# Hybrid decode step: order of the state mixers, their PSUM banks, and a float32 part of the out projection

## The chip, the cores and the metric

The kernel runs on one core of one Trainium2 chip. The metric is the device time of one execution in microseconds (us). The kernel is written with a tile framework: the program text offers instructions with priorities, and a scheduler fixes one static order per engine before the launch. The engines are PE (matrix products), DVE (vector), ACT (scalar functions), POOL (general) and SP (which here issues DMAs).

## The reference

A two-layer hybrid network advances 272 prompt tokens (16 meta tokens and 256) and 8 decode tokens, 280 columns in all. Each layer is a gated feed-forward, then three mixers side by side, then a second feed-forward:

```python
h = x + 0.5 * swiglu(rmsnorm(x, ffn1_norm), ...)
proj = rmsnorm(h, mix_norm) @ w_in
u_s5, p_rwkv, x_lru, g_lru = jnp.split(proj, [...], axis=-1)
o_s5, ...   = s5_group_mixer(u_s5, ...)       # diagonal state space, then a gate z @ glu_w
o_rwkv, ... = rwkv7_group_mixer(p_rwkv, ...)  # S = S*w + sa*(kk*a) + v*k over the tokens, head norm, bonus, gate
o_lru, ...  = rglru_group_mixer(x_lru, g_lru, ...)  # conv of 4, gated linear recurrence, h * gelu(gb)
mix = jnp.concatenate([o_s5, o_rwkv, o_lru], axis=-1) @ w_out
h = h + mix
h = h + 0.5 * swiglu(rmsnorm(h, ffn2_norm), ...)
```

The model width is 1024 (8 row tiles of 128). The mixers' width is 384 for S5 (tiles 0 to 2 of the out projection's rows), 384 for RWKV (tiles 3 to 5) and 256 for RG-LRU (tiles 6 and 7).

## The kernel before

Everything is kept transposed, features on partitions and the 280 tokens on columns. A float32 weight product is made of three faster fp32r matmuls: a weight piece is loaded into a staging buffer (`wpiece`, L180 to L193; five buffers with the tag `stg`), ACT rounds it to `whi` (L191), DVE or POOL takes the remainder `wlo` (L192), and `gemm` (L195 to L203) adds whi·xh, whi·xl and wlo·xh in one PSUM bank, where xh and xl are the same two parts of the activations. PSUM's eight banks are four groups: psa has three, psb two, psc two, psd one. A bank is taken in turn within its group, and the next taker waits until the last has been read.

`mixers` (L1241) runs once per layer. `proj(i)` makes one of 18 tiles of the in projection, 8 x 3 matmuls into a psa bank. In the order of the program text stand:

- RWKV's keys, decay and weighted keys, then `within` for the products EM (i = 0), masked by DVE, one head half in psb and the other in psc;
- `do_i`: the inverses' first stage. `rwkv_inverse` (L902) inverts the triangular 16 x 16 blocks of all chunks on DVE (L922 to L956, between stream transpositions of AD), and yields;
- `do_v`, `do_x`: the values, the bonus and the gate's input;
- `do_o`: `within` again, for the products EO (i = 1);
- `do_s`: three S5 tiles of the in projection and their rearrangement by DMA; `do_l`: four RG-LRU tiles, and the loads of the S5 gate's weights `gw` (tag `stg`);
- `do_C`: `rwkv_chunks` (L1010), a plain function: keys by token, `solve` for the chunks, the inverses' second stage in two groups (L961 to L1008, taken by `next(inv)`), the state over five chunks, the head norms;
- S5's groups and closes (L668, L706) with `do_L` among them: `lru` (L759), conv, two gate products (L777, L780), Tanh, Exp and Sqrt on ACT, the scan (L794), the gelu (L727), the output tile `gb` (L799) and its split in two parts (`split_o`);
- `do_t`: `s5_tail`, three banks of three float32 gate matmuls (L752) on S5's `u`, and their split.

The out projection (L1491 to L1505) then makes eight tiles of rows k = 0, 1, 2, 6, 7 (15 matmuls each, psc) and eight of k = 3, 4, 5 (9 each). DVE adds each into the residual `hres` (L1505), and the second feed-forward begins with its norm.

Of the kernel before, what the change touches and what calls it, by code (L numbers as in the profile page):

```python
# [74 lines left out]
def tile_hybrid_decode(ctx, tc, *args):  # L75
# [683 lines left out]
    def lru(l, mp, cb, gb, s5, pc, hc, out_tile):  # L759
# [28 lines left out]
        for t in range(2):  # L788
# [11 lines left out]
            split_o(6 + t, gb[:, t])  # L800
# [209 lines left out]
    def rwkv_chunks(l, mp, p0, p2, inv, TT, RA, RAw, BK, BK0, EM, EO, vv, vvw, bon, xg, gu, pcl, yd, pc, decode):  # L1010


# [125 lines left out]
        def outputs(c, Tp):  # L1138
# [9 lines left out]
            for hp in range(3):  # L1148
                for h in range(2):
                    yr = slice(64 * h, 64 * h + n)  # L1150
                    PE.matmul(py[yr, hp], EO[:, c, hp, h, 0:n], UV[:, c, hp, h], start=(c == 0), stop=True,
                              skip_group_check=c > 0)
# [3 lines left out]
        st = Tc = out = None  # L1156
        by_token0()
        solve(0)
        next(decode)
        for c, (t0, n) in enumerate(CHUNKS):  # L1160
            if c:

                cs = slice(t0, t0 + n)
                G.tensor_tensor(RA[:, :, :, cs], RA[:, :, :, cs],
                                pcl[:, :, c - 1].unsqueeze(2).unsqueeze(3).to_broadcast([P, 3, 2, n]), op=MUL)
# [3 lines left out]
        keys_by_token(1)  # L1169
# [5 lines left out]
        for c in range(2, 5):  # L1175
            keys_by_token(c)
        for c, (t0, n) in enumerate(CHUNKS):
            bt, uv = bts[c], UV[:, c]
# [57 lines left out]
        return final_state  # L1236
# [4 lines left out]
    def mixers(l, s5, acc, cols, gnext):  # L1241
# [17 lines left out]
        def proj(i):  # L1259
            w = wpiece(w_in[:, :, i * P:i * P + P])  # L1260
            pt = psA()
            gemm(pt[:, :NT], w, ks, xh, xl, ks, True, True)
            return pt
# [27 lines left out]
        def shifted(i, out, ti, act=False):  # L1291

            pt = proj(ti)
# [18 lines left out]
        def decay(hp):  # L1312

            hs = slice(hp * P, hp * P + P)
            pz = psB()
            PE.matmul(pz[:, :NT], lw[0:64, hs], xw[0:64], start=True, stop=True)
            s1 = dk()
            S.activation(s1, pz[:, :NT], AF.Tanh, bias=hc('rwkv_w0', hp), scale=0.5)
            S.activation(s1, s1, AF.Copy, bias=1.0)
            pz = psB()  # L1320
            PE.matmul(pz[:, :NT], lw[64:128, hs], xw[64:128], start=True, stop=True)
            at = dk()
            S.activation(at, pz[:, :NT], AF.Tanh, bias=hc('rwkv_a0', hp), scale=0.5)
# [16 lines left out]
        def keys():  # L1340
# [3 lines left out]
            for hp in range(3):  # L1344
                kt.append(rk())
                shifted(3 + hp, kt[hp], 6 + hp)
                sq.append(rk())
                S.activation(sq[hp], kt[hp], AF.Square, scale=pc('rwkv_k_k', hp))
                for g, m, cs in tok(NT):
                    c = 6 * g + 2 * hp  # L1350
                    PE.matmul(pz[:m, c:c + 2], sq[hp][:, cs], bd1[:, 0:P:64], start=True, stop=True)
# [80 lines left out]
        def do_l():  # L1432
            for t in range(2):
                pt = proj(14 + t)
# [59 lines left out]
        n = cols.stop - cols.start  # L1494
# [100 lines left out]
```

## Time and profile before

| | |
|---|---|
| median of 3 runs | 1278.68 us (1273.01 to 1279.05) |
| profiled execution | 1279.83 us, its span 1278.0 us |
| mean granted PE clock | 0.958 |
| busy, us | PE 1222.5, DVE 999.5, ACT 690.2, POOL 348.9 |
| layer 0, mixers' projections | to 327.9 us |
| layer 0, out projection | 406.5 to 431.3 us |
| layer 1, first S5 gate product of the last five | 1032.1 us |

A row of the timeline gives the start of an instruction in us from the span's start, how long it took, its engine, line and operation with out and in by the program's names, and in brackets the idle time of the engine just before it with the instruction that ended this idle time. Matmuls overlap, so their durations add up to more than the time between their starts. A float32 matmul has two records (x2 is one matmul). The granted clock is a share of PE's full 2.4 GHz; 0.5 is 1.2 GHz.

### The profile page before, as it was taken

The page shows a single profiled execution, that of the slowest core. Times are in us where ns is not written, and L with a number is a line of the kernel's source. Part 1 is how long each engine was busy: PE and PEld are TensorE (multiplying, and loading weights), DVE is VectorE, ACT ScalarE, POOL GpSimd, SP SyncE. Part 2 cuts the span into 40 slices and gives each one's busy share as a digit, 9 for nine tenths or more (in the row PEclk, how much of TensorE's full clock was granted, in tenths as well). Part 3 has the DMA queues.
Part 4 walks back from the last instruction along what each step waited for, and adds up shares of the span by engine and source line. Part 5 has one row for each costly group of instructions (what it writes and reads, how often), then busy time and mean ns, then how long its engine had stood idle before and what let it go on. Part 6 is the DMA issues. An engine that isn't in the chain of part 4 may idle for free.

```text
span 1278.0 us, 29512 instructions
## 1 busy us (share of the span) xinstructions
PE 1222.5 (96%) x10744; PEld 1161.3 (91%) x10744; DVE 999.5 (78%) x2395; ACT 690.2 (54%) x1489; POOL 348.9 (27%) x619
## 2 busy tenths in 40 slices
PE   7999899999898999989999999999999989999997
PEld 6999899988776999989998999998888779999996
DVE  7999976679687799998667878756876778987854
ACT  4556565564355555656544555556633656555552
POOL 2104852033443210385207000001615332500000
PEclk9999999989897999989999999999995989999998
DMA  7665455524311756535578665654333028866662
GB/s 187 168 182 156 132 148 154 164 83 117 92 33 50 187 160 190 156 104 169 161 185 225 194 171 167 178 168 142 105 86 93 3 83 223 237 193 177 179 187 79
DMA packets 376911, 187.49 MB, mean 147 GB/s; under 512 B 45532, under 2 KB 375352, under 8 KB 376766
## 3 DMA queue, kind: packets, MB, share of 16 engines
q1 hardware_dynamic: 376430, 184.47, 52.0%
q8 instruction: 84, 1.38, 0.4%
q10 hardware_dynamic: 336, 1.15, 0.3%
q14 instruction: 61, 0.50, 0.1%
HBM read 181.31 MB, written 3.37 MB: 145 GB/s over the span
## 4 chain that ended last, share of the span: by engine, by line
PE 79%; DVE 11%; DMA 4%; issue 2%; ACT 2%; POOL 1%; SPq 0%; DVEq 0%; ACTq 0%; POOLq 0%
PE psa L202 11%; PE psa L201 11%; PE psa L200 10%; PE psc L201 6%; PE psc L202 6%; PE psc L200 6%; PE psb L202 6%; PE psb L200 6%; PE psb L201 6%; DVE wlo L192 3%; DMA stg<-in_ffn_w_gate_dram 2%; DMA stg<-in_ffn_w_up_dram 1%; PE psc L752 1%; PE psc L677 1%; PE psc L715 1%
## 5 line engine op out<-in xcount | busy, mean ns | idle before, releaser
L191 ACT ACTIVATE whi<-stg 128x512 fp32r<-128x512 f32 (+2 forms) x664 | 399.3, 608 | 354.4 <-PE psa L201 116.1
L192 DVE TENSOR_TENSOR wlo<-stg,whi 128x512 fp32r<-128x512 f32 (+2 forms) x640 | 445.8, 700 | 129.0 <-PE psa L202 35.3
L202 PE MATMUL psa<-xh,wlo 128*128 128x280 f32 (+1 forms) x930 | 275.7, 298 | 5.0 <-DVE wlo L192 4.5
L200 PE MATMUL psa<-xh,whi 128*128 128x280 f32 (+1 forms) x930 | 273.7, 295 | 2.8 <-DVE ts L1296 2.1
L201 PE MATMUL psa<-xl,whi 128*128 128x280 f32 (+1 forms) x930 | 272.9, 294 | 0.0
L202 PEld LDWEIGHTS psa<-xh,wlo 128*128 128x128 f32 x930 | 176.4, 190 | 10.4 <-DVE wlo L192 7.9
L200 PEld LDWEIGHTS psa<-xh,whi 128*128 128x128 f32 x930 | 177.5, 191 | 5.4 <-DVE ts L1296 2.3
L201 PEld LDWEIGHTS psa<-xl,whi 128*128 128x128 f32 x930 | 177.0, 190 | 1.8 <-issue 1.0
L202 PE MATMUL psc<-xh,wlo 128*128 128x280 f32 (+1 forms) x498 | 145.1, 292 | 1.8 <-DVE wlo L192 1.8
L200 PE MATMUL psc<-xh,whi 128*128 128x280 f32 (+1 forms) x498 | 145.2, 292 | 1.0 <-ACT xh L264 0.5
L201 PE MATMUL psc<-xl,whi 128*128 128x280 f32 (+1 forms) x498 | 144.8, 291 | 1.1 <-DVE xl L265 0.7
L202 PE MATMUL psb<-xh,wlo 128*128 128x280 f32 (+1 forms) x396 | 115.6, 292 | 1.3 <-DVE wlo L192 1.3
L200 PE MATMUL psb<-xh,whi 128*128 128x280 f32 (+1 forms) x396 | 115.8, 292 | 0.2 <-ACT whi L191 0.2
L201 PE MATMUL psb<-xl,whi 128*128 128x280 f32 (+1 forms) x396 | 115.3, 291 | 0.0
L202 PEld LDWEIGHTS psc<-xh,wlo 128*128 128x128 f32 x498 | 94.0, 189 | 2.8 <-DVE wlo L192 2.7
L200 PEld LDWEIGHTS psc<-xh,whi 128*128 128x128 f32 x498 | 94.0, 189 | 2.3 <-ACT xh L738 0.8
L201 PEld LDWEIGHTS psc<-xl,whi 128*128 128x128 f32 x498 | 94.0, 189 | 1.9 <-DVE xl L265 1.0
L202 PEld LDWEIGHTS psb<-xh,wlo 128*128 128x128 f32 x396 | 74.9, 189 | 2.2 <-DVE wlo L192 2.2
L200 PE MATMUL psb<-hh,whi 128*128 128x280 f32 (+1 forms) x264 | 76.7, 291 | 0.0
L200 PE MATMUL psa<-hh,whi 128*128 128x280 f32 (+1 forms) x264 | 76.6, 290 | 0.0
L202 PE MATMUL psb<-hh,wlo 128*128 128x280 f32 (+1 forms) x264 | 76.5, 290 | 0.0
L202 PE MATMUL psa<-hh,wlo 128*128 128x280 f32 (+1 forms) x264 | 76.5, 290 | 0.0
(618 smaller groups left out, 2743.3 us busy)
## 6 DMA issues: line engine op xcount, KB each, us to landing
stg<-in_ffn_w_gate_dram SPq DMA_DIRECT2D x176, 256.0 KB
stg<-in_ffn_w_up_dram SPq DMA_DIRECT2D x176, 256.0 KB
stg<-in_ffn_w_down_dram SPq DMA_DIRECT2D x160, 256.0 KB
stg<-in_w_in_dram SPq DMA_DIRECT2D x72, 256.0 KB
stg<-in_w_out_dram SPq DMA_DIRECT2D x32, 192.0 KB
bc<-ds SPq DMA_DIRECT2D x24, 192.0 KB
stg<-in_ffn_w_down_dram SPq DMA_DIRECT2D x32, 128.0 KB
bc<-ds SPq DMA_DIRECT2D x12, 256.0 KB
```

What stands on the lines that cost most here:

```text
L191: S.activation(hi[:, :kc], st[:, :kc], AF.Copy)
L192: (eng or V).tensor_tensor(lo[:, :kc], st[:, :kc], hi[:, :kc].bitcast(F32), op=SUB)
L200: PE.matmul(out, w[wk[i]][0], ah[:, k], start=(first and i == 0), stop=False)
L201: PE.matmul(out, w[wk[i]][0], al[:, k], start=False, stop=False)
L202: im = PE.matmul(out, w[wk[i]][1], ah[:, k], start=False, stop=(last and i == n - 1))
L677: PE.matmul(px[r][:, a], s5['xbt'][:, 4 * T + a, r], u4[:, 4 * T + a, 8:16 + NQ], start=True, stop=True)
L715: PE.matmul(py[32 * i:32 * i + 32, c0:c0 + n], w, x[:, o:NQ + ND], start=(m == 0), stop=(m == 2), skip_group_check=True, tile_position=(0, ...
L752: PE.matmul(pz[:, :NT], gw[k][:, j], z5[:, k, 0:NT], start=(k == 0), stop=(k == 2))
```

## The change

It has three parts.

First, `rwkv_chunks` becomes a generator in three pieces. Its first piece (chunk 0's keys and solution, the inverses' second stage, chunk 1's solution, the values by token) is offered right behind `do_x`, ahead of `do_o`, `do_s` and `do_l`. Its second piece (decode, the other keys, chunks 0 to 2) is offered behind `do_o`. Its last piece (chunks 3 and 4, the head norms) is offered behind `do_t`, in a block of high priority. The scaling of RA by pcl is split in the two kinds of rows, so that each stands where its kind is needed.

Second, the S5 and RG-LRU projections and the third key tile take psc banks instead of psa banks, and the decay takes both its psb banks before it reads the first.

Third, RG-LRU's rows of the out projection (k = 6, 7) are made by plain float32 matmuls from `gb` and unsplit weights: four tiles `ow` with the tag `stg` are loaded in `do_l` by eight DMAs of 128 KB, and ahead of `do_t` sixteen matmuls (L1510) and eight adds into `hres` (L1511) take the place of 48 fp32r matmuls. The loop of the out projection then has k = 0, 1, 2 and k = 3, 4, 5, each tile with one weight piece, and DVE takes every remainder. `gb` is not split any more.

```diff
@@ lru
             V.scalar_tensor_tensor(gb[:, t], gb[:, t], 0.5, h, op0=MUL, op1=MUL)
-            split_o(6 + t, gb[:, t])
@@ rwkv_chunks
         by_token0()
         solve(0)
-        next(decode)
-        for c, (t0, n) in enumerate(CHUNKS):
-            if c:
-
-                cs = slice(t0, t0 + n)
-                G.tensor_tensor(RA[:, :, :, cs], RA[:, :, :, cs],
-                                pcl[:, :, c - 1].unsqueeze(2).unsqueeze(3).to_broadcast([P, 3, 2, n]), op=MUL)
+        enter(0)
         for w in range(2):
             values_by_token(w)
             first_by_token(w)
-        keys_by_token(1)
         next(inv)
         solve(1)
         next(inv)
         for w in range(2, 5):
             values_by_token(w)
-        for c in range(2, 5):
+        yield
+        next(decode)
+        enter(1)
+        for c in range(1, 5):
             keys_by_token(c)
         for c, (t0, n) in enumerate(CHUNKS):
+            if c == 3:
+                yield
...
@@ mixers
-        def proj(i):
+        def proj(i, bank=psA):
             w = wpiece(w_in[:, :, i * P:i * P + P])
-            pt = psA()
+            pt = bank()
...
-            pz = psB()
+
+            pz, pa = psB(), psB()
             PE.matmul(pz[:, :NT], lw[0:64, hs], xw[0:64], start=True, stop=True)
+            PE.matmul(pa[:, :NT], lw[64:128, hs], xw[64:128], start=True, stop=True)
...
-                shifted(3 + hp, kt[hp], 6 + hp)
+                shifted(3 + hp, kt[hp], 6 + hp, bank=psC if hp == 2 else psA)
...
-                pt = proj(14 + t)
+                pt = proj(14 + t, psC)
...
-                pt = proj(16 + t)
+                pt = proj(16 + t, psC)
                 V.scalar_tensor_tensor(gb[:, t], pt[:, :NT], KR, rs, op0=MUL, op1=MUL)
+
+            R['lw'] = [wp.tile([P, 4, P], F32, name="ow", tag="stg", bufs=NBW[0]) for _ in range(KD // 2)]
+            for i, w in enumerate(R['lw']):
+                for q in range(2):
+                    nc.sync.dma_start(w[:, 2 * q:2 * q + 2], w_out[:, 6:8, (2 * i + q) * P:(2 * i + q) * P + P])
             R['gw'] = glu_weights(l)
...
-                pt = proj(T)
+                pt = proj(T, psC)
...
         do_x()
+        chain = do_C()
+        next(chain)
         do_o()
+        next(chain)
         do_s()
         do_l()
-        do_C()
...
         s5_close(s5, u5, R['u4'], 2, R['2'])
+
+        n = cols.stop - cols.start
+        for j in range(KD):
+            pt = psC()
+            for k in range(2):
+                PE.matmul(pt[:, :n], R['lw'][j // 2][:, 2 * (j % 2) + k], gb[:, k, cols], start=(k == 0), stop=(k == 1))
+            V.tensor_tensor(hres[:, j, cols], pt[:, :n], hres[:, j, cols], op=ADD)
         do_t()
+        with tc.high_priority():
+            next(chain)
...
-        OPE = [G, G, V]
-        for kk in ([0, 1, 2, 6, 7], [3, 4, 5]):
-            rw = len(kk) == 3
+        for kk in ([0, 1, 2], [3, 4, 5]):
+            rw = kk[0] == 3
...
-                w = wpiece([w_out[:, 3:6, js]] if rw else [w_out[:, 0:3, js], w_out[:, 6:8, js]], V if rw else OPE[j % len(OPE)])
+                w = wpiece(w_out[:, kk[0]:kk[0] + 3, js])
```

PE around the start of the inverses' second stage (the first L970), layer 0. In the kernel before all projections stand ahead of these rows; psa, psb, psc and psd are the bank groups, L1046 brings values and keys to token rows, L677 are S5's groups, L1087 is chunk 0's solution:

```order
L177 MATMUL psa<-ident,BK_3697 16x64
L177 MATMUL psa<-ident,vv 16x64
L970 MATMUL psb<-AD,EM 32x16 x12
L677 MATMUL psc<-u_4597,xbt 128x76 [waits DMAHW4_49,DMAHW3_49,DMAHW5_49,DMAHW2_49,Pool_49]
L677 MATMUL psc<-u_4597,xbt 128x76 [waits DMAHW6_49,DMAHW7_49,DMAHW1_49,DMAHW0_49]
L1046 MATMUL psa<-ident,vv 128x128 [waits DVE_49]
L1046 MATMUL psa<-ident,vv 128x128 x2
L677 MATMUL psc<-u_4597,xbt 128x76 [waits DMAHW4_49,DMAHW5_49,DMAHW3_49,DMAHW2_49]
L677 MATMUL psc<-u_4597,xbt 128x76 [waits DMAHW6_49,DMAHW7_49,DMAHW1_49,DMAHW0_49]
L677 MATMUL psc<-u_4597,xbt 128x76 x4
L1087 MATMUL psd<-UV,EM 16x64 [waits Activation_49]
```

And in the changed kernel, where the second stage is at L969, the transpositions at L1047 and chunk 0's solution at L1088:

```order
L202 MATMUL psc<-xh,wlo 128x280
L969 MATMUL psb<-AD,EM 32x16 [waits DVE_49,Activation_49]
L969 MATMUL psb<-AD,EM 32x16 [waits Activation_49]
L969 MATMUL psb<-AD,EM 32x16 x3
L1047 MATMUL psa<-ident,RA 128x128 [waits Activation_49]
L1088 MATMUL psd<-UV,EM 16x64 [waits Activation_49]
L1047 MATMUL psa<-ident,RA 128x128
L1088 MATMUL psd<-UV,EM 16x64 [waits Activation_49]
L1088 MATMUL psd<-UV,EM 16x64 x4
L1047 MATMUL psa<-ident,RA 128x128
L1047 MATMUL psa<-ident,vv 128x128 x3
L1047 MATMUL psa<-ident,RA 128x128 x3
```

The second stage now stands behind two S5 tiles (48 matmuls in psc, the last of them in the first row) and ahead of the other five (120 matmuls, the first of which follows two rows further down), and S5's groups come behind all of these.

DVE at the end of RG-LRU's chain, layer 0, before. L727 is the gelu, L799 writes `gb`, L739 splits it, and L1127 to L1133 and the lines with smy and smd are head norms:

```order
L1127 SCALAR_TENSOR_TENSOR bon<-psa,pv,bon 128x64 [waits PE_49]
L1127 SCALAR_TENSOR_TENSOR bon<-psa,pv,bon 128x64 x2
L163 TENSOR_TENSOR smyrt<-smyry 128x3 [waits DVE_49]
L165 SCALAR_TENSOR_TENSOR smdrt<-smdrt 128x24 [waits DVE_49]
L799 SCALAR_TENSOR_TENSOR gb<-gb,tf 128x280
L727 SCALAR_TENSOR_TENSOR gb<-tf,gb 128x280 [waits Activation_49]
L1131 TENSOR_TENSOR bon<-bon,vv 128x3x64 [waits DVE_49]
L164 TENSOR_TENSOR smyrt<-smyrt,smyv 128x3 [waits DVE_49]
L166 SCALAR_TENSOR_TENSOR smdry<-smdrt,smdry 128x24 [waits DVE_49]
L727 SCALAR_TENSOR_TENSOR u_4121<-tf 128x280 [waits Activation_49]
L799 SCALAR_TENSOR_TENSOR gb<-gb,tf 128x280 [waits DVE_49]
L739 SCALAR_TENSOR_TENSOR xl<-gb,xh 128x280 [waits Activation_49]
```

And in the changed kernel, where L1132 and L1134 are the last rows of the head norms and L1511 the new adds:

```order
L1134 TENSOR_TENSOR xl<-bon,xh 128x3x72 [waits Activation_49]
L790 SCALAR_TENSOR_TENSOR ta<-tf,ta 128x280 [waits Activation_49] x2
L792 SCALAR_TENSOR_TENSOR tf<-tf 128x280 [waits Pool_49]
L794 SCALAR_TENSOR_TENSOR tf<-tf 128x272 [waits DVE_49]
L792 SCALAR_TENSOR_TENSOR tf<-tf 128x280 [waits Pool_49]
L794 SCALAR_TENSOR_TENSOR tf<-tf 128x272 [waits DVE_49]
L727 SCALAR_TENSOR_TENSOR gb<-tf,gb 128x280 [waits Activation_49]
L799 SCALAR_TENSOR_TENSOR gb<-gb,tf 128x280 [waits DVE_49]
L727 SCALAR_TENSOR_TENSOR gb<-tf,gb 128x280 [waits Activation_49]
L799 SCALAR_TENSOR_TENSOR gb<-gb,tf 128x280 [waits DVE_49]
L727 SCALAR_TENSOR_TENSOR u_4121<-tf 128x280 [waits Activation_49]
L1511 TENSOR_TENSOR hres<-psc,hres 128x280 [waits PE_49] x8
```

The steps of RG-LRU's chain from L790 on stand alone, behind all head norms, where they were mixed with them before.

PE from RG-LRU's output to the out projection, layer 0, before. L752 are the S5 gate's products, L175 and L177 transpose outputs of the head norms, L200 is the first matmul of the out projection:

```order
L752 MATMUL psc<-u_4121,gw 128x280 [waits DMAHW4_49,DVE_49]
L752 MATMUL psc<-u_4121,gw 128x280
L752 MATMUL psc<-u_4121,gw 128x280 [waits Activation_49]
L752 MATMUL psc<-u_4121,gw 128x280 x2
L175 MATMUL psa<-ident,EM 64x64 [waits DVE_49]
L177 MATMUL psa<-ident,EM 64x64
L175 MATMUL psa<-ident,EM 64x64
L177 MATMUL psa<-ident,EM 64x64
L175 MATMUL psa<-ident,EM 64x64
L177 MATMUL psa<-ident,EM 64x64
L200 MATMUL psc<-xh,whi 128x280 [waits Activation_49]
L201 MATMUL psc<-xl,whi 128x280 [waits DVE_49]
```

And in the changed kernel, where the first row is the last pair's first of the sixteen L1510:

```order
L1510 MATMUL psc<-gb,ow 128x280 [waits DMAHW5_49,DVE_49]
L1510 MATMUL psc<-gb,ow 128x280
L752 MATMUL psc<-u_4121,gw 128x280 [waits DMAHW6_49,DVE_49]
L752 MATMUL psc<-u_4121,gw 128x280 [waits DMAHW7_49]
L752 MATMUL psc<-u_4121,gw 128x280 [waits DMAHW0_49]
L752 MATMUL psc<-u_4121,gw 128x280 [waits DVE_49]
L752 MATMUL psc<-u_4121,gw 128x280 x2
L752 MATMUL psc<-u_4121,gw 128x280 [waits Activation_49]
L752 MATMUL psc<-u_4121,gw 128x280 x2
L200 MATMUL psc<-xh,whi 128x280 [waits Activation_49]
L201 MATMUL psc<-xl,whi 128x280 [waits DVE_49]
```

All sixteen float32 matmuls stand ahead of all nine of L752 (four of which stood further up before), and no transposition is left among them. On SP, the eight loads of `ow` stand where the first pieces of the out projection's weights were: the loads of the second and third `gw` and of all those pieces now stand behind a wait for PE, which is done with `ow` at L1510.

## Rows read from the trace of the kernel before

**Rows 1.** The page, part 1: busy us, share of the span, instructions.

```profile
PE 1222.5 (96%) x10744; PEld 1161.3 (91%) x10744; DVE 999.5 (78%) x2395; ACT 690.2 (54%) x1489; POOL 348.9 (27%) x619
```

**Rows 2.** The page, part 4: the chain that ended last, by engine.

```profile
PE 79%; DVE 11%; DMA 4%; issue 2%; ACT 2%; POOL 1%; SPq 0%; DVEq 0%; ACTq 0%; POOLq 0%
```

**Rows 3.** Busy time by stretch; columns stand in the first line, stretches in us.

```profile
core 0: us, PE busy (x) PEld busy (x) DVE busy (x) ACT busy (x) POOL busy (x), PEclk, DMA share, GB/s
303.00:327.90 24.90, 24.90 (x199) 23.17 (x197) 21.91 (x58) 7.12 (x12) 5.98 (x9) 1.00 0.25 64
327.90:361.50 33.60, 28.90 (x658) 24.41 (x657) 23.48 (x55) 13.45 (x41) 16.92 (x30) 0.80 0.39 106
361.50:406.50 45.00, 39.27 (x555) 28.17 (x553) 35.98 (x116) 28.59 (x72) 17.35 (x27) 0.81 0.06 17
406.50:431.30 24.80, 24.46 (x187) 24.01 (x187) 16.31 (x40) 14.82 (x33) 6.96 (x8) 1.00 0.58 166
957.00:1005.00 48.00, 46.83 (x876) 39.92 (x876) 29.43 (x68) 20.58 (x62) 22.86 (x41) 0.61 0.26 72
```

**Rows 4.** PE timeline: start, duration, line, operation, count, idle before it and its releaser.

```profile
249.66 0.93 PE L285 MATMUL psd<-ident,nrm 128*128 128x128 f32 x6
...
251.64 0.40 PE L200 MATMUL psa<-xh,whi 128*128 128x280 f32 x1 [1.05 <-DVE ts L1296]
...
330.45 0.38 PE L970 MATMUL psb<-AD,EM 16*32 16x16 f32 x24
...
361.04 0.52 PE L1046 MATMUL psa<-ident,vv 128*64 128x128 f32 x3
...
381.68 0.74 PE L777 MATMUL psc<-tf,lg 128*128 128x280 f32 x2
...
382.26 0.64 PE L780 MATMUL psc<-tf,lg 128*128 128x280 f32 x2
...
400.41 4.85 PE L752 MATMUL psc<-u,gw 128*128 128x280 f32 x10 [2.44 <-DVE u L727]
...
406.48 0.40 PE L200 MATMUL psc<-xh,whi 128*128 128x280 f32 x1
...
880.85 0.40 PE L200 MATMUL psa<-xh,whi 128*128 128x280 f32 x1 [1.05 <-DVE ts L1296]
...
1032.11 4.74 PE L752 MATMUL psc<-u,gw 128*128 128x280 f32 x10 [2.76 <-DVE u L727]
```

**Rows 5.** DVE timeline, same columns.

```profile
302.40 0.67 DVE L192 TENSOR_TENSOR wlo<-stg,whi 128x512 fp32r<-128x512 f32 x1
...
303.00 1.08 DVE L922 STREAM_TRANSPOSE wk<-AD 128x512 f32<-128x512 f32 x1
...
312.42 1.71 DVE L943 TENSOR_TENSOR wk<-DD,XI 128x512 f32<-128x512 f32 x1
...
322.74 1.10 DVE L955 STREAM_TRANSPOSE AD<-wk 128x512 f32<-128x512 f32 x1
...
400.27 0.44 DVE L799 SCALAR_TENSOR_TENSOR gb<-gb,tf 128x280 f32<-128x280 f32 x1
...
433.78 0.44 DVE L1505 TENSOR_TENSOR hres<-psc,hres 128x280 f32<-128x280 f32 x1
...
1031.98 0.43 DVE L799 SCALAR_TENSOR_TENSOR gb<-gb,tf 128x280 f32<-128x280 f32 x1
...
1064.64 0.43 DVE L1505 TENSOR_TENSOR hres<-psc,hres 128x264 f32<-128x264 f32 x1
```

**Rows 6.** DVE alone by stretch: busy time, clock, DMA share, GB/s.

```profile
303.00:400.35 97.35, 76.52 (x207) 0.87 0.22 57
361.50:400.35 38.85, 31.13 (x95) 0.84 0.04 11
```

**Rows 7.** ACT timeline, RG-LRU gates of layer 0.

```profile
382.93 0.49 ACT L781 ACTIVATE tf<-psc,h 128x280 f32<-128x280 f32 x1
...
385.00 1.28 ACT L787 ACT_TABLE_LOAD   x1
...
386.30 0.76 ACT L787 ACTIVATE ta<-ta 128x280 f32<-128x280 f32 x2
```

**Rows 8.** DVE groups by line and form, layer 0 mixers: busy, mean ns, idle before.

```profile
L1127 DVE SCALAR_TENSOR_TENSOR bon<-psa,pv,bon 128x64 f32<-128x64 f32 x6 | 1.3, 278 | 1.7 <-PE psa L177 1.7
```

More of the change, by code (lines that the diff above doesn't have):

```diff
@@ L1008, in rwkv_inverse, with rwkv_chunks @@
             yield
-    def rwkv_chunks(l, mp, p0, p2, inv, TT, RA, RAw, BK, BK0, EM, EO, vv, vvw, bon, xg, gu, pcl, yd, pc, decode):
+    def rwkv_chunks(l, mp, p0, R, inv, TT, RA, RAw, BK, BK0, EM, vv, vvw, bon, xg, gu, pcl, yd, pc, decode):
+        p2 = R['p2']
         UV = p0.tile([P, 5, 3, 2, 64], F32, name="UV", tag="uv")
@@ L1150, in outputs @@
                     yr = slice(64 * h, 64 * h + n)
-                    PE.matmul(py[yr, hp], EO[:, c, hp, h, 0:n], UV[:, c, hp, h], start=(c == 0), stop=True,
+                    PE.matmul(py[yr, hp], R['EO'][:, c, hp, h, 0:n], UV[:, c, hp, h], start=(c == 0), stop=True,
                               skip_group_check=c > 0)
@@ L1156, in rwkv_chunks, with enter @@
         st = Tc = out = None
+        def enter(i):
+            for c, (t0, n) in enumerate(CHUNKS):
+                if c:
+                    cs = slice(t0, t0 + n)
+                    G.tensor_tensor(RA[:, :, i, cs], RA[:, :, i, cs],
+                                    pcl[:, :, c - 1].unsqueeze(2).to_broadcast([P, 3, n]), op=MUL)
         by_token0()
         solve(0)
-        next(decode)
-        for c, (t0, n) in enumerate(CHUNKS):
-            if c:
-                cs = slice(t0, t0 + n)
-                G.tensor_tensor(RA[:, :, :, cs], RA[:, :, :, cs],
-                                pcl[:, :, c - 1].unsqueeze(2).unsqueeze(3).to_broadcast([P, 3, 2, n]), op=MUL)
+        enter(0)
         for w in range(2):
@@ L1234, in final_state @@
             nc.sync.dma_start(D['p_rwkv'][l][0].rearrange("(a h) v k -> (h v) a k", h=2), sf)
-        return final_state
+        R['fs'] = final_state
+        yield
     NU = 12
@@ L1289, in mixers, with shifted @@
         dst_ = mp.tile([P, 15, ND], F32, name="dst", tag="sd")
-        def shifted(i, out, ti, act=False):
-            pt = proj(ti)
+        def shifted(i, out, ti, act=False, bank=psA):
+            pt = proj(ti, bank)
             pb = tmp("s", 4, p1)
@@ L1319, in decay @@
             S.activation(s1, s1, AF.Copy, bias=1.0)
-            pz = psB()
-            PE.matmul(pz[:, :NT], lw[64:128, hs], xw[64:128], start=True, stop=True)
             at = dk()
-            S.activation(at, pz[:, :NT], AF.Tanh, bias=hc('rwkv_a0', hp), scale=0.5)
+            S.activation(at, pa[:, :NT], AF.Tanh, bias=hc('rwkv_a0', hp), scale=0.5)
             af = dk()
@@ L1465, in do_C @@
             G.tensor_copy(vd, vv[:, :, NPR:NT])
-            R['fs'] = rwkv_chunks(l, mp, p0, R['p2'], R['inv'], R['TT'], RA, RAw, BK, BK0, EM, R['EO'], vv, vvw, bon, xg, gu, pcl, yd, pc,
-                        rwkv_decode(l, mp, ds, vv, dots, ys, yd))
+            return rwkv_chunks(l, mp, p0, R, R['inv'], R['TT'], RA, RAw, BK, BK0, EM, vv, vvw, bon, xg, gu, pcl, yd, pc,
+                               rwkv_decode(l, mp, ds, vv, dots, ys, yd))
         def do_L():
@@ L1488, in mixers @@
         s5_close(s5, u5, R['u4'], 2, R['2'])
+        n = cols.stop - cols.start
[4 more added lines that the diff above has]
+            V.tensor_tensor(hres[:, j, cols], pt[:, :n], hres[:, j, cols], op=ADD)
         do_t()
+        with tc.high_priority():
+            next(chain)
         ro, rc = R['ro'], R['rc']
         acc2 = new_acc()
-        n = cols.stop - cols.start
-        OPE = [G, G, V]
-        for kk in ([0, 1, 2, 6, 7], [3, 4, 5]):
-            rw = len(kk) == 3
+        for kk in ([0, 1, 2], [3, 4, 5]):
+            rw = kk[0] == 3
             if rw:
```

## Prediction

> **What bounds the kernel now.** I read the page's first part and the chain before anything else: PE is busy 96% of the span [rows 1] and the chain that ended last lies on it for 79% [rows 2]. That average hides the only stretch that the change touches, so the next view is the table by stretches [rows 3]. In layer 0's mixers, from 327.9 to 406.5 us, PE still counts as busy, but with small products, and at a granted clock of 0.80 and 0.81: the projections have ended and nothing large is left to fill it. DVE there is busy 23.48 of 33.60 and 35.98 of 45.00 us. From 406.5 the out projection runs dense at clock 1.00: 192 matmuls of 280 columns in 24.80 us, 0.129 each. Layer 1 is colder: 0.61 from 957 to 1005.
>
> The single instructions show what that stretch waits for. PE's order has the last projection at 327.9, the inverses' second stage from 330.45, the last of its values at about 361.5, then five gate matmuls (L752) from 400.41, released by DVE's `u`, and the out projection at 406.48 [rows 4]. On DVE, the inverses' first stage lasts from 303.00 to about 323.8, and RG-LRU's second output tile `gb` is written by 400.71 [rows 5]. Between 303.00 and 400.35 DVE is busy 76.52 of 97.35 us, in the last part 31.13 of 38.85 [rows 6]. So this stretch is a chain DVE, PE, ACT, DVE in which DVE has most of the work, and its end, `gb` and `u`, opens the out projection. A gain needs that end earlier by more than the tail behind it gets longer.
>
> **Third key tile in an own bank.** PE waits 1.05 us at 251.64 for a bank, behind the norm's transposes at 249.66 [rows 4]; another bank lets these 24 matmuls run there. -1.0 us per layer (0 to -1.05). The decay's two banks cost nothing on the path: the rows show no PE wait there, and the cover is the projections beside it.
>
> **Earlier first stage.** In the new order two splits (0.6 apart) and one S5 evacuation (0.65) no longer stand ahead of the first transposition: it starts at 303.00 - 1.85, about 301.2 [rows 5]. Six splits (3.6), three evacuations (1.8) and 0.4 of idle leave its 20.8 us: AD is ready at about 301.2 + 14.9 = 316.1, where before PE reached it at 330.45.
>
> **PE behind it.** The S5 tiles now use the two psc banks that hold the EO products. DVE frees these in its own order, behind 1.71 us multiplies such as that at 312.42 [rows 5]. So PE stands from about 302 to 308.5, runs 48 matmuls (6.2) to 314.7 and waits 1.4 more for AD. Since AD comes last, I count the wait for the banks as nothing; were AD early or the masks later, it would cost up to its 6.5 us per layer, which is a rival below. The Trainium skill (Perfetto Trace Analysis, Matmuls) says that independent matmul groups should rotate through different PSUM banks so that the evacuation of one overlaps the next group's matmuls; here seven tiles lose three banks for two shared ones, so it speaks against this part, and by it alone the sum would be 1303.5 instead of 1290.5. Behind AD 120 matmuls follow (15.5 us at 0.129), with some 14.5 us of second stage, solves and transposes, about half of the 28.90 that PE spends between 327.9 and 361.5 [rows 3]; S5's groups are the other half. The last projection and the inverses end at 316.1 + 30.0, about 346.2: 15 us before the 361.5 of now.
>
> **What DVE still owes.** The order has 23 more instructions between the first transposition and the last `u` than before: two splits, one S5 evacuation, the last chunk's bonus products and small norm steps, which stood ahead or behind. At 1.4 for the splits and about 0.18 for each of the others that is 5.2 us, so 76.5 + 5.2 = 81.7. What stands ahead of the last projection's evacuation is 33.5 of it. S5's groups, the chunks, the head norms and RG-LRU, 48.2 us, now all come behind 346.2. Idle comes on top. RG-LRU's gates for the second tile stand behind all head norms on PE, ACT and DVE, so nothing covers their latency any more: 1.2 on PE (381.68 to 382.9 [rows 4]), 4.1 on ACT from 382.93 to 387.06, a table load of 1.28 among it [rows 7], and some 1.2 of POOL: 6.5 us. For the chunks and norms I keep 4.1, about half of the 7.7 that DVE idles from 361.50 to 400.35 [rows 6]; the waits for the bonus transposes, 1.7 in one group alone [rows 8], are of this kind. `gb` is ready at 346.2 + 48.2 + 10.6, about 405.0 to 405.2, against 400.71: **+4.5 us**. Layer 1 lies 629.2 later by its key tile (880.85 against 251.64 [rows 4]): 1034.4, where its cold stretch now gives 1032.41 [rows 5]: **+2.0**. The bounds: no idle but RG-LRU's 6.5, filled from the start, gives 301.2 + 81.7 + 6.5 = 389.4; twice the chunks' idle gives 409.3.
>
> **The tail behind `gb`.** Before, it takes from 400.71 to the last add into `hres`, which ends at 434.22: 33.5 us in layer 0; in layer 1 from 1032.41 to 1065.07, 32.7 [rows 5]. Now the sixteen float32 matmuls stand ahead of all gate matmuls and can't start before `gb`. One takes 0.97 at the low clock (five in 4.85 at 400.41) and half, 0.49, at the high one; a pair at 381.68 shows 0.58 [rows 4]. PE has waited long before them, so I take four at 0.97 and twelve at 0.49: 9.8. Bounds: 7.8 (all at the high clock) and 15.5 (none). Nine gate matmuls follow, 4.5; the wait for the first split of their output, 1.4 (1.2 lie between 405.26 and 406.48 now [rows 4], with transpositions in them); 144 matmuls, 18.6; to the end of the last add 2.9, as from 431.3 to 434.22 now. Sum 37.2: +3.7 in layer 0. In layer 1, with 264 columns, the sixteen, the 144 and the rest come to about 36.4, again **+3.7**. The 48 matmuls removed (6.2 us) are worth less than the sixteen cost, and of the nine gate matmuls, four of which had run before 400.41, all stand behind `gb` now.
>
> **Off the path.** ACT loses eight weight splits and the two of `gb`; DVE gets eight adds and all lo-parts, and loses those two tiles' lo-parts; POOL loses six splits. DVE is busy 16.31 of 24.80 us in the out projection [rows 3], which covers them. On SP eight 128 KB loads go into four of the five staging buffers, and two gate tiles and the out projection's first weights wait until the sixteen matmuls free them. The first weights then have 10 us until the out projection; I cost that at 0, and up to 2 us per layer if landing, split and remainder take longer.
>
> **Sum.** Layer 0: -1.0 + 4.5 + 3.7 = 7.2. Layer 1: -1.0 + 2.0 + 3.7 = 4.7. Together 11.9 on the profiled execution's 1279.83: 1291.7. That execution stands 1.15 above the median of the runs, so 1290.5 us.
>
> **Rivals.** *DVE's holes fill: faster.* S5 and RG-LRU work beside the chunks, with no idle but RG-LRU's latency. That puts `gb` 15.8 earlier than forecast: -8.6 in layer 0, -11.1 in layer 1, 1260 profiled. It decides at 7.2 of the 15.8 in layer 0; at three quarters (11.9 each) the time is 1267.9, or 1266.7 against the median. For it: 20.8 us of idle are there [rows 6], and PE is free. Against: S5's first group is offered only behind the last projection, and the RG-LRU tail is alone. The Trainium skill (Perfetto Trace Analysis, Optimization Strategy) says that where the most-contended engine changes over time, interleaving these regimes may improve the time. Here the projections (PE) and the inverses (DVE) are such regimes; no row of the kernel before shows them interleaved.
>
> *It cancels.* Half of the 15.8 is saved, 7.9 per layer: 1279.83 + 11.9 - 15.8 = 1275.9, 1274.8 against the median; between a third and a half it is within the noise, so I put this case at 1278.
>
> *The wait for the banks counts.* The EO masks come behind AD's transposition or the first stage ends sooner, and PE's 6.5 us move everything behind: 1291.7 + 13.0 = 1304.7, 1303.5 against the median. For it: the 1.71 us multiplies [rows 5]; against: the masks stand ahead of AD's transposition in DVE's order.
>
> *A cold, starved tail: slower still.* All sixteen at the low clock (+5.7 per layer) and weights 1.5 late: 11.9 + 14.4, 1306 profiled, 1305. For it: 0.61 in layer 1's stretch [rows 3] and five cold gate matmuls in both layers (1032.11 too [rows 4]). That the change does not do what it says is excluded by the order of its instructions.
>
> **How the numbers follow.** The forecast has 0.42, with its own range from 1285 to 1300. The holes filling has 0.22 (1258 to 1272), the cancelling case 0.22 (1272.3 to 1285), the wait for the banks 0.04, the cold tail 0.10. About 0.5% (6.4 us) is what a measurement of this kernel tells from no change; so faster 0.22, same 0.22, slower 0.56. The range reaches from 1264 to 1305: it leaves out some 0.08 below and 0.06 above.
>
> **What would show it.** Right: PE idle near 302 to 308 behind the EO products; the second stage starting at about 316; the last projection at about 346; `gb` at 404 to 406 less the shift of the key tile; DVE waits in the last 10 us before it; sixteen matmuls in 9 to 11 us, and 37 us from `gb` to the last add. Wrong: `gb` before 396, or a tail under 34 us.

## The result and the profile after

The changed kernel takes 1318.28 us (median of 4 runs, 1317.47 to 1320.09) against 1277.43 for the kernel before in 4 runs: a ratio of 1.033 by the record (95% interval 1.0304 to 1.0356; the two medians alone give 1.032). The profiled executions differ by 1317.99 - 1279.83 = 38.2 us. The forecast was slower by 11.9, 1290.5 us, and 1318 lies above its range of 1264 to 1305: the direction held, the size did not.

From the page's first two parts: the first row is the changed kernel's and answers to [rows 1]. The clock rows, 40 slices of the span, are the changed kernel's and then that of before. They show where the clock falls: slices 9 to 13 and 29 to 33, the mixers of the two layers, in most of them lower than before.

```profile
PE 1231.5 (94%) x10712; PEld 1165.6 (89%) x10712; DVE 1009.1 (77%) x2415; ACT 684.2 (52%) x1469; POOL 325.5 (25%) x603
...
PEclk9999999987875999999999999999888779999998
...
PEclk9999999989897999989999999999995989999998
```

The table by stretches of the changed kernel, layer 0, with the columns of [rows 3]:

```profile
303.00:318.00 15.00, 15.00 (x85) 13.44 (x84) 14.52 (x38) 4.88 (x10) 0.42 (x1) 0.66 0.07 19
318.00:331.00 13.00, 13.00 (x199) 11.38 (x200) 7.65 (x23) 6.75 (x18) 1.65 (x5) 1.00 0.42 111
331.00:353.80 22.80, 22.80 (x408) 21.34 (x408) 10.56 (x26) 3.60 (x11) 3.50 (x8) 0.78 0.40 106
353.80:394.20 40.40, 34.49 (x591) 28.05 (x590) 30.76 (x82) 16.21 (x45) 18.86 (x34) 0.84 0.10 27
394.20:421.20 27.00, 12.09 (x124) 8.25 (x125) 15.84 (x64) 13.44 (x27) 7.02 (x13) 0.56 0.03 6
421.20:459.10 37.90, 35.83 (x206) 30.54 (x205) 25.65 (x60) 18.75 (x43) 0.00 (x0) 0.94 0.47 137
```

Two stretches stand out. From 303 to 318 PE gets through 85 records only, at clock 0.66, and few weights arrive (19 GB/s). The same stretch before:

```profile
303.00:318.00 15.00, 15.00 (x123) 13.41 (x122) 14.18 (x41) 4.59 (x8) 3.96 (x4) 1.00 0.28 77
```

From 394 to 421 DVE is busy 15.84 of 27.00 us and PE 12.09, at clock 0.56: up to 407 the last head norms with RG-LRU's conv, then the rest of RG-LRU's chain alone. The end of the mixers was cold before too (0.55 from 390 to 406.5), but there DVE was busy 13.99 of 16.50 us. The first stretch is also in SP's waits of the changed kernel, 300 to 330 us (total, times, longest). Weight loads stand 19.3 us behind one split, so the weight buffers were full and nothing drained them; before, the longest such wait is 7.1 us and all of them 14.0.

```profile
SPq L188 <- DVE wlo L192: 25.0, 4, 19.3
```

PE and DVE of the changed kernel, layer 0, columns of [rows 4]:

```profile
251.65 0.93 PE L285 MATMUL psd<-ident,nrm 128*128 128x128 f32 x6
...
310.17 0.60 PE L200 MATMUL psc<-xh,whi 128*128 128x280 f32 x1
...
317.90 0.29 PE L969 MATMUL psb<-AD,EM 16*32 16x16 f32 x10
...
351.72 0.76 PE L1003 MATMUL psa<-TT,Z 32*32 32x32 f32 x36
...
407.12 1.27 PE L777 MATMUL psc<-tf,lg 128*128 128x280 f32 x2 [2.10 <-DVE tf L773]
...
420.43 10.48 PE L1510 MATMUL psc<-gb,ow 128*128 128x280 f32 x32 [8.14 <-ACT tf L726]
...
430.74 4.41 PE L752 MATMUL psc<-u,gw 128*128 128x280 f32 x18
...
436.02 0.40 PE L200 MATMUL psc<-xh,whi 128*128 128x280 f32 x1 [0.87 <-ACT ta L754]
```

```profile
302.89 1.06 DVE L921 STREAM_TRANSPOSE wk<-AD 128x512 f32<-128x512 f32 x1
...
315.49 1.14 DVE L954 STREAM_TRANSPOSE AD<-wk 128x512 f32<-128x512 f32 x1
...
354.09 0.45 DVE L1451 SCALAR_TENSOR_TENSOR gb<-psc,nry 128x280 f32<-128x280 f32 x1 [0.65 <-PE psc L202]
...
393.19 0.92 DVE L1128 SCALAR_TENSOR_TENSOR bon<-psa,pv,bon 128x144 f32<-128x144 f32 x3 [3.80 <-PE psa L177]
...
412.25 0.81 DVE L790 SCALAR_TENSOR_TENSOR ta<-tf,ta 128x280 f32<-128x280 f32 x2 [4.58 <-ACT ta L787]
...
419.39 0.45 DVE L727 SCALAR_TENSOR_TENSOR gb<-tf,gb 128x280 f32<-128x280 f32 x1 [2.75 <-ACT tf L726]
...
420.72 0.45 DVE L799 SCALAR_TENSOR_TENSOR gb<-gb,tf 128x280 f32<-128x280 f32 x1
...
458.69 0.44 DVE L1528 TENSOR_TENSOR hres<-psc,hres 128x280 f32<-128x280 f32 x1
```

In what follows times are counted from the mixers' norm (the transpositions at 249.66 before [rows 4], 251.65 now), since its place varies between runs, 247.5 to 253.5 us over all kernels here, with the same program ahead of it. From the norm to the last add into the residual, layer 0 now takes 207.5 instead of 184.6 us and layer 1 201.1 instead of 186.2: 22.9 + 14.9 = 37.8, the whole loss.

| us behind the norm, layer 0 (layer 1) | before | after |
|---|---|---|
| first transposition of AD starts | 53.3 (50.9) | 51.2 (51.5) |
| inverses' second stage starts | 80.8 (78.4) | 66.2 (66.8) |
| inverses end | 109.4 (111.1) | 100.8 (100.0) |
| last projection evacuated | 78.8 (76.4) | 102.9 (102.1) |
| RG-LRU's second output tile written | 151.0 (153.6) | 169.5 (165.5) |
| last add into the residual | 184.6 (186.2) | 207.5 (201.1) |

The inverses do come 9 to 11 us earlier. The projections of S5 and RG-LRU come 24 to 26 later, and RG-LRU's output and the last add are late with them.

One count will be needed below: how many matmuls L201 (one of the three fp32r products; a tile has eight) run between the first transposition of AD and the last evacuation of a projection. It is a row of the view by stretches for that line alone (length, busy, count, clock, DMA share, GB/s). Before:

```profile
303.00:328.47 25.47, 13.30 (x45) 1.00 0.25 63
```

After, where 56 is all seven S5 and RG-LRU tiles (in the kernel before, 11 of the 56 had run ahead of the first transposition):

```profile
302.89:354.54 51.65, 18.14 (x56) 0.80 0.30 80
```

### The profile page after: what moved, and what is told of

It is laid out like the page before. It is cut to its first block, busy times and chain, and to the rows that moved or that the text cites. A ratio compares the mean times of both kernels' runs of the same rounds, so it can differ in the third digit from the quotient of the medians.

```text
span 1316.3 us, 29422 instructions
## 1 busy us (share of the span) xinstructions
PE 1231.5 (94%) x10712; PEld 1165.6 (89%) x10712; DVE 1009.1 (77%) x2415; ACT 684.2 (52%) x1469; POOL 325.5 (25%) x603
## 5 line engine op out<-in xcount | busy, mean ns | idle before, releaser
L202 PE MATMUL psa<-xh,wlo 128*128 128x280 f32 (+1 forms) x802 | 234.2, 293 | 2.2 <-DVE wlo L192 2.0
L200 PE MATMUL psa<-xh,whi 128*128 128x280 f32 (+1 forms) x802 | 234.6, 293 | 0.7 <-ACT whi L191 0.7
L201 PE MATMUL psa<-xl,whi 128*128 128x280 f32 (+1 forms) x802 | 232.5, 291 | 0.0
L200 PE MATMUL psc<-xh,whi 128*128 128x280 f32 (+1 forms) x594 | 177.5, 300 | 3.9 <-ACT ta L754 1.8
L201 PE MATMUL psc<-xl,whi 128*128 128x280 f32 (+1 forms) x594 | 176.3, 297 | 1.9 <-DVE xl L265 1.0
L202 PE MATMUL psc<-xh,wlo 128*128 128x280 f32 (+1 forms) x594 | 176.0, 297 | 1.8 <-DVE wlo L192 1.8
L202 PEld LDWEIGHTS psa<-xh,wlo 128*128 128x128 f32 x802 | 150.7, 188 | 5.6 <-DVE wlo L192 4.6
L200 PEld LDWEIGHTS psa<-xh,whi 128*128 128x128 f32 x802 | 151.4, 189 | 3.5 <-issue 2.2
L201 PEld LDWEIGHTS psa<-xl,whi 128*128 128x128 f32 x802 | 151.1, 189 | 0.8 <-issue 0.7
L200 PEld LDWEIGHTS psc<-xh,whi 128*128 128x128 f32 x594 | 114.5, 193 | 7.1 <-ACT ta L754 2.7
L201 PEld LDWEIGHTS psc<-xl,whi 128*128 128x128 f32 x594 | 115.0, 194 | 3.2 <-DVE xl L739 1.8
L200 PE MATMUL psb<-xh,whi 128*128 128x280 f32 (+1 forms) x396 | 115.0, 291 | 0.0
L201 PE MATMUL psb<-xl,whi 128*128 128x280 f32 (+1 forms) x396 | 114.8, 290 | 0.0
L200 PE MATMUL psb<-hh,whi 128*128 128x280 f32 (+1 forms) x264 | 76.8, 291 | 0.0
L200 PE MATMUL psa<-hh,whi 128*128 128x280 f32 (+1 forms) x264 | 76.6, 290 | 0.0
L201 PE MATMUL psb<-hl,whi 128*128 128x280 f32 (+1 forms) x264 | 76.6, 290 | 0.0
```

Source lines behind the costliest of these rows:

```text
L200: PE.matmul(out, w[wk[i]][0], ah[:, k], start=(first and i == 0), stop=False)
L201: PE.matmul(out, w[wk[i]][0], al[:, k], start=False, stop=False)
L202: im = PE.matmul(out, w[wk[i]][1], ah[:, k], start=False, stop=(last and i == n - 1))
```

## The experiments

Each run gives its median time, its ratio to the kernel before as run beside it, and in brackets the 95% interval of that ratio. Times "behind the norm" are of layer 0 unless both layers are given.

Theory A: the last chunk piece's priority pushes RG-LRU's chain behind the head norms. Theory B: projections among the inverses' second stage are what costs, by way of the banks. Theory C: the float32 products. Later ones are D (late projections, whatever made them late), F (psc shared with EO) against G (the chunks in pieces), and H (the turn of the banks keeps the tiles from filling PE's holes) against I (two banks are too few).

### Four parts taken out or alone

**e1**, the changed kernel:

```diff
-        with tc.high_priority():
-            next(chain)
+        next(chain)
```

> The changed kernel with the last piece of the RWKV chunks (chunks 3 and 4, head norms) offered at the same place but without high priority. Theory A (RG-LRU's chain comes last because that piece goes ahead of it; the new output of RG-LRU is 18.5 us later than before, from the norm of layer 0, and 12.0 in layer 1, and the chain's own waits cause most of that): about 1300 us, 18 less than the changed kernel's 1318, with RG-LRU's second output tile 8 to 10 us earlier in each layer. Theory B (the projections among the inverses' second stage cost the time: the last projection ends at 353.8 instead of 327.9 us): no change, 1315 to 1321. Theory C (the float32 products cost most of it): no change.

1308.93 us, 1.0249 (1.0208 to 1.0291): 9 us of the 41. On DVE RG-LRU's conv starts 134.7 instead of 142.5 us behind the norm and its second tile is written at 164.7, 4.8 less, where A expected 8 to 10; in layer 1 it is 163.8, 1.7 less. A is half right: the mechanism is there, and small.

**e2**, the changed kernel:

```diff
-                pt = proj(T, psC)
+                pt = proj(T)
```

and the same for `proj(14 + t)`, `proj(16 + t)` and the third key tile.

> The changed kernel with all projections in the psa banks again (the third key tile too). Theory B (the shared psc banks hold the projections up, PE stalls behind the masks and then runs at the low clock): the last projection of layer 0 ends 6 to 8 us earlier, at about 346, and the time is about 1303 us. Theory A (the place of RG-LRU's chain decides): within 5 us of 1318, since that chain still comes last in DVE's order. Theory C: 1318.

1338.04 us, 1.0491 (1.0446 to 1.0536), a miss for all: 20 us slower than the change. The last projection is evacuated 125.6 us behind the norm. In the new order the tiles are offered behind a piece that itself takes psa, for the second group of the inverses and all transpositions, and stand behind it in psa's turn: the first S5 tile is evacuated 105.0 us behind the norm, against 65.5 in the change.

**e3**, the kernel before with `ow`, L1510, L1511 and the shorter loop of the out projection alone:

> The kernel before with only the third part of the change: RG-LRU's rows of the out projection as sixteen float32 matmuls from unsplit weights, adds ahead of the S5 gate. Theory C: 7 us per layer or more, 1291 us and up. Theories A and B: only the measured longer tail, 4.4 and 2.9 us (from the second output tile to the last add into the residual), so about 1285 us, and less if RG-LRU's chain moves ahead of the head norms in DVE's order.

1273.80 us, 0.999 (0.9963 to 1.0018). C falls. A and B had 1285, and less if RG-LRU's chain moves ahead in DVE's order; it does. Its output is written 140.1 and 142.5 us behind the norm, and the sixteen products run before the head norms have ended (161.1 and 170.0).

**e4**, the changed kernel with `split_o(6 + t, ...)`, the five-tile loop and no `ow`:

> The changed kernel without its third part: RG-LRU's output is split and the out projection takes five row tiles by fp32r matmuls as before; order and banks as changed. Theories A and B: the tail gets back its 7.3 us, so about 1311 us. Theory C: 1285 us or less.

1311.78 us, 1.0272 (1.0225 to 1.0319): the 6.5 us of the longer tail, as A and B expected.

### The order and the banks apart

**e5**, the changed kernel with the order put back and all else kept (the loads of `ow` and `gw` in a function of their own):

```diff
-        chain = do_C()
-        next(chain)
-        do_o()
-        next(chain)
-        do_s()
-        do_l()
+        do_o()
+        do_s()
+        do_l()
+        do_w()
+        chain = do_C()
+        next(chain)
+        next(chain)
```

> The changed kernel with one thing put back: the EO products, the S5 and the RG-LRU projections (with the loads behind them) are offered ahead of the first piece of the RWKV chunks, which holds the inverses' second stage. The three pieces, the priority of the last, the banks and the float32 products stay. Theory D (the cost is that the last projection is evacuated 103 us behind the mixers' norm instead of 79, while DVE's S5 and RG-LRU work of some 60 us can only start behind it): 1275 us, within 6 of the kernel before, RG-LRU's output 140 to 151 us behind the norm. Theory A (priority of the last piece): still 1305 or more, since the priority is there. Theory F (the psc banks themselves hold the projections up): above 1285.

1311.14 us, 1.0276 (1.0252 to 1.03), a miss for D's 1275. With the projections first the kernel is hardly better, so the new order is not the main cost. The last projection is still late, 90.4 behind the norm.

**e6**, `do_l()` ahead of the first piece, `do_s()` behind:

> The changed kernel with RG-LRU's four projection tiles ahead of the chunks' first piece and the S5 tiles behind it (the loads of unsplit and gate weights behind both). Theory D, if S5's late start is what counts: 1305 to 1320 us, as changed, since S5's groups begin no earlier. Theory D, if RG-LRU's late start is what counts: 1285 to 1295.

1343.46 us, 1.0537 (1.0513 to 1.0562), a miss: 25 us slower than the change. The last projection stands at 105.2 and RG-LRU's output at 183.9 behind the norm. RG-LRU's own tiles are evacuated by 68.3, but on DVE its conv only starts at 162.1, near the end of the head norms (164.6). So early RG-LRU tiles alone gain nothing here; why the scheduler puts the conv so late was not tried.

**e7**, `do_s()` ahead, `do_l()` behind:

> The changed kernel with the three S5 tiles ahead of the chunks' first piece and RG-LRU's four tiles behind it. Theory D, if S5's late start is what counts: 1285 to 1300 us, S5's first group some 15 us earlier. Theory D, if RG-LRU's is: 1310 to 1320, as changed.

1316.81 us, 1.0311 (1.029 to 1.0332): S5's tiles are evacuated at 64.5 instead of 74.2, yet nothing is won. RG-LRU's (102.9) are as late as in the change.

**e8**, the kernel before with e3's part and

```diff
-                shifted(3 + hp, kt[hp], 6 + hp)
+                shifted(3 + hp, kt[hp], 6 + hp, bank=psC if hp == 2 else psA)
```

and the decay's two banks:

> The kernel before with the float32 products of the third part and, of the second part, the third key tile's own bank and the decay's two banks; nothing reordered, the S5 and RG-LRU projections in psa. By the 1.05 us wait that goes in each layer: 2 us below the float32 products alone (1273.8), so 1270 to 1273 us, 0.2 to 0.5% under the kernel before. If a later wait takes it up: 1273 to 1277.

1268.30 us, 0.9937 (0.9915 to 0.9959): faster than both kernels, by more than the wait that was known. The last projection is evacuated 72.1 behind the norm.

**e9**, e5 with the S5 and RG-LRU tiles in psa:

> As the run with the projections first (1311 us), with the S5 and RG-LRU tiles in psa banks again; the third key tile keeps its psc bank. Theory F (the seven tiles wait for the two psc banks that the EO products hold, the weight buffers stay full behind them and SP's loads stop for 21 us): 1268 to 1280 us, the last projection evacuated 72 to 79 us behind the norm instead of 90. Theory G (the chunks in three pieces with priority for the last are what costs): 1300 or more.

1279.35 us, 1.0021 (0.999 to 1.0053), with the last projection evacuated at 72.5, as F expected. Against e5's 1311.14 the banks of seven tiles cost 31.8 us.

**e10**, e8 with those seven tiles in psc, nothing reordered:

> The kernel before with the float32 products and the whole second part (third key tile, S5 and RG-LRU tiles in psc, decay's two banks), nothing reordered. It differs from the run at 1268.3 us by the banks of seven tiles alone. Theory F: 1295 to 1311 us, the last projection evacuated near 90 us behind the norm, little DMA traffic in the 15 us behind the first transposition. Theory G: 1268 to 1275.

1305.89 us, 1.0217 (1.0183 to 1.025). Against e8 the same edit costs 37.6 us. F holds and G falls: this edit alone is nearly as dear as the whole change. The stretches 250 to 303 and 303 to 318 (columns of [rows 3]), e8:

```profile
250.00:303.00 53.00, 51.26 (x427) 45.48 (x426) 43.21 (x97) 36.86 (x105) 23.27 (x53) 1.00 0.44 124
303.00:318.00 15.00, 15.00 (x121) 13.32 (x121) 14.17 (x42) 4.40 (x8) 4.16 (x6) 1.00 0.33 79
```

and e10:

```profile
250.00:303.00 53.00, 48.66 (x373) 40.13 (x374) 40.63 (x89) 36.02 (x104) 22.95 (x53) 0.85 0.34 98
303.00:318.00 15.00, 15.00 (x80) 13.23 (x80) 12.76 (x35) 3.42 (x8) 4.02 (x5) 0.50 0.06 16
```

The loss begins ahead of 303: e10 has 54 PE records fewer there and a clock of 0.85, then half the clock and few weights (16 GB/s). In e8 the three S5 tiles are evacuated 44.2, 47.4 and 52.3 us behind the norm, ahead of the first transposition of AD (52.8); in e10 at 69.7, 74.2 and 77.4, behind it (51.2).

**e11** and **e12**, the change and e5, with one half of the EO products in psa:

```diff
+        bh = psA if i else psC
-            pg = [bk()[:, :192].rearrange("p (u t) -> p u t", u=3) for bk in (psB, psC)]
+            pg = [bk()[:, :192].rearrange("p (u t) -> p u t", u=3) for bk in (psB, bh)]
```

> The changed kernel with one half of the EO products in psa banks instead of psc, so that the S5 and RG-LRU tiles share no bank with them. Theory F: the wait at 302 to 308 us goes, 10 us or more per layer, 1290 to 1300 us. Theory G or the new order itself: 1310 to 1318.

> As the run with the projections first (1311 us), with one half of the EO products in psa instead of psc. Theory F: 1270 to 1280 us, as with the tiles in psa. Theory G: 1305 to 1311.

1305.95 (1.0224) and 1300.40 us (1.0171): 12 and 11 us back, so both miss what F expected; e12 gets about a third of it. EM is still in psc, and 55 and 56 of the L201 still come behind the first transposition of AD. So sharing with EO is a part only.

### Psc for the tiles alone

**e13** is e10, **e14** the whole change, both with

```diff
-            pg = [bk()[:, :192].rearrange("p (u t) -> p u t", u=3) for bk in (psB, psC)]
+            pg = [bk()[:, :192].rearrange("p (u t) -> p u t", u=3) for bk in (psB, psB)]
```

for EM and EO alike (and the same for the 16-row products).

> As the run with all banks of the change and nothing reordered (1305.9 us), but EM and EO take psb for both halves, so that from the third key tile on psc holds S5 and RG-LRU tiles alone. Theory H (what counts is the turn of the banks: in psc these tiles come behind EM and EO and can't fill PE's holes ahead of the first stage): nearly all of their matmuls run ahead of the first transposition of AD, the last is evacuated 55 to 72 us behind the norm instead of 90, and the time is 1265 to 1285 us. Theory I (two banks are too few for seven tiles): 1300 or more.

1292.58 us, 1.0102 (1.0068 to 1.0136), between the two: nearly all tiles run ahead (3 of the L201 remain, the last evacuated at 67.4), but EM and EO in two banks instead of four delay AD to 64.4, the inverses to 119.8 and the head norms to 176.5, and now RWKV's chain is late.

> The whole change, with EM and EO in psb for both halves. Theory H, and the new order harmless without the wait: 1265 to 1285 us, as the run before it. If the new order costs something of its own (the inverses' second stage and the projections among each other): 1290 to 1310. Theory I: 1310 or more.

1280.28 us, 1.0021 (1.0 to 1.0043): 38 of the 41 us come back with this one edit, order, priority and float32 products untouched. H holds and I falls: two banks are enough for seven tiles when EM and EO do not stand ahead of them in their turn. The edit moves EM and EO and not the tiles, and so it has a price of its own, as in e13: AD's first transposition starts at 61.7 instead of 51.2. The last projection is evacuated at 66.3 all the same, instead of 102.9. The count by stretches for L201, e14:

```profile
311.67:316.30 4.63, 2.19 (x8) 1.00 0.70 203
```

and the same kernel's stretches 250 to 318, where PE stays at full clock and weights at 120 GB/s:

```profile
250.00:303.00 53.00, 52.27 (x427) 45.59 (x426) 43.03 (x94) 37.41 (x106) 24.32 (x55) 1.00 0.45 122
303.00:318.00 15.00, 14.82 (x121) 13.95 (x120) 10.35 (x35) 4.94 (x9) 2.62 (x6) 1.00 0.48 124
```

Behind the projections its clock falls as well, and the time is that of the kernel before even so. A cold stretch alone does not bring a loss like that of the change:

```profile
331.00:354.00 23.00, 21.12 (x472) 18.03 (x473) 15.43 (x38) 7.63 (x24) 8.59 (x17) 0.61 0.20 49
```

e13 and e14 differ by the first part of the change (the pieces, their order, the priority): it is worth 12 us where the tiles can run early, and the inverses end at 110.6 instead of 119.8 us behind the norm. Between e10 and the change the same part costs 12 us where they can't, of which the order alone is 7 (e5).

**e15**, the kernel before with e8's bank edits alone:

> The kernel before with the third key tile in psc and the decay's two banks, nothing else. If these banks make the gain of the run at 1268.3 us and the float32 products nothing: 1266 to 1271 us. If the gain needs both: 1274 to 1278.

1267.97 us, 0.9911 (0.9876 to 0.9946): the gain of e8 is that of the banks. This is the fastest kernel of the study. Its count (e8 and e9 have 29 as well) and its tail on DVE:

```profile
306.32:325.63 19.31, 8.65 (x29) 1.00 0.32 85
```

```profile
387.94 0.83 DVE L799 SCALAR_TENSOR_TENSOR gb<-gb,tf 128x280 f32<-128x280 f32 x1
...
429.39 0.44 DVE L1504 TENSOR_TENSOR hres<-psc,hres 128x280 f32<-128x280 f32 x1
```

Layer 0 from the norm (253.49) to the last add takes 176.3 us, against 184.6 before; layer 1 takes 179.2, against 186.2. How much of this is the key tile's bank and how much the decay's was not tried.

## Why the prediction was right or wrong

- **First stage**: right, in part by luck. AD was forecast ready at 316.1, which with the key tile's 1.0 off is 65.4 behind the norm; measured 316.63, 65.0. It starts 0.7 later than forecast and takes 13.7 us instead of 14.9.
- **Tail behind `gb`**: right. Forecast 37.2 and +3.7 per layer; measured 38.0 and 35.6, +4.4 and +2.9. The sixteen products take 10.3 us (9.8 forecast), the nine of L752 4.4 (4.5).
- **"PE behind it", 30.0 us**: failed. The order was the forecast one, 48 matmuls of the tiles ahead of the second stage and 120 behind, but the term was too small. From AD to the last projection's evacuation it is 354.54 - 316.63 = 37.9. The 48 do not end ahead of AD: they start at 310.17 and end at 317.98, 1.3 behind it. Then, from start to start in PE's timeline, the 120 matmuls take 19.3 us (15.5 forecast; the clock is 0.78 from 331 to 353.8) and the steps between them 16.7 (14.5 forecast). In these are 4.2 us of EO products (L896, psb), which the forecast had not counted behind AD.
- **"What DVE still owes", idle 10.6**: failed. DVE's content was right (79.42 us busy from the first transposition to `gb`, 81.7 forecast), the idle time was not: 38.9 instead of 22.3 over the whole, and 20.8 instead of 10.6 behind the last projection. In DVE's rows by stretch of the changed kernel:

```profile
302.89:421.17 118.28, 79.42 (x229) 0.76 0.17 46
353.80:421.17 67.37, 46.58 (x144) 0.73 0.07 18
```

and its waits from 302.89 to 421.17:

```profile
DVE bon L1128 <- PE psa L177: 6.5, 3, 3.8
DVE ta L790 <- ACT ta L787: 4.6, 1, 4.6
DVE TT L1006 <- PE psa L1003: 3.6, 1, 3.6
```

  Behind the last projection, the waits of RG-LRU's chain from L790 on come to 8.0 us (4.6 of them above), where 6.5 was forecast. That leaves 12.8 for the chunks and norms, where I kept 4.1. The waits for the bonus transposes alone are 6.5, and I had argued from a group with 1.7 [rows 8]. `gb` came 18.5 us later against the norm in layer 0 and 11.9 in layer 1, where 3.5 and 1.0 were forecast; together 25.9 of the 26.3 by which the forecast fell short.
- **The wait for the banks**: this is the step that stands behind both. I took it as nothing "since AD comes last", left it as a rival with 0.04, and priced that rival by PE's standing time from 302 to 308 us alone. The second stage starts at 317.90, when the 48 matmuls are done, so AD did not come last. The price is not the 1.3 us of that: the runs give 31.8 (e5 to e9) and 37.6 us (e8 to e10) for the banks of the seven tiles. In the changed kernel itself e14 takes back 38.0. There DVE idles 76.53 - 57.27 = 19.3 us from the first transposition to `gb` (311.67 to 388.20), instead of 38.9. What I didn't see is what the tiles did before: in psa they ran ahead of AD's first transposition (11 of the 56 L201) and beside the first stage (45), with PE at clock 1.00. In psc they stand behind EM and EO in the turn, so all 56 come behind the first transposition, PE's clock is 0.66 from 303 to 318, and the weight buffers stay full. How the 38 us divide between late tiles, clock and weights was not tried. The rule of the Trainium skill that I had cited (Perfetto Trace Analysis, Matmuls: rotate independent groups through different banks) agrees in its direction with these two pairs of runs, but not with e2, where three banks are 20 us slower than two. It gives no price, and counting banks would not have done, since e14 uses the same two for the tiles.
- **Third key tile, -1.0 us per layer**: too small. With the decay's banks it is worth 10.3 us (e15). The 1.05 us wait [rows 4] is gone there in both layers, which is at most 2.1 of it. Beside this, 16 more L201 run ahead of AD's first transposition (29 behind it instead of 45); that they make the rest is likely, but not shown.
- **"It cancels" and "DVE's holes fill"**: the first part of the change, which was to fill the holes, is worth 12 us in e14 against e13 and costs 12 in the change against e10. The banks decide which. I wrote that no row of the kernel before shows the projections and the inverses interleaved. That was a wrong reading of [rows 3]: from 303.00 to 327.90 PE is busy, mostly with projections, for 24.90 us, and DVE, with the first stage among its work, for 21.91. The interleaving that the Trainium skill speaks of (Perfetto Trace Analysis, Optimization Strategy) may improve the time, it says. Here it did not by itself: the changed kernel runs 120 of the tiles' matmuls between the steps of the second stage, and e14, where all but 8 of the 56 L201 run ahead of the first transposition, is 38 us faster.
- **The cold tail**: 394.20 to 421.20 is cold (0.56), but the sixteen products took 10.3 us, not 15.5, and the out projection did not wait for weights: its 0.87 us wait at 436.02 is for ACT's `ta`.

## What to carry to other kernels

When work is moved to other banks, ask what that work filled while it waited for nothing: a low-priority tile is useful in holes only if every earlier taker in its group's turn is done by then. Read the turn from the program's order, group by group, and count how many matmuls lie on each side of the next long wait. A wait that looks as if another one covers it can still hold up the weight stream behind it.

## What was not expected

Edits of bank names alone, with the same matmuls, moved the time by 38 us in either direction (e10, e14). The three effects came together: PE's clock at 0.50 from 303 to 318 us in e10, DMA at 16 GB/s in the same 15 us, and 19.3 us in which SP could issue no weight load in the changed kernel. The group with three banks (psa, e2) made the new order worse, not better, by 20 us.
